# The last third of the last product of a decoder step, in seven products instead of eight

## The chip, the core and the metric

One core of a Trainium2 chip. The metric is device time in microseconds for one execution of the whole program. The engines are TensorE (PE: matmuls and transposes), VectorE (DVE), ScalarE (ACT) and GpSimd (POOL); SyncE (SP) issues every DMA of this kernel, in one queue and in order.

## The reference

One step of a one-layer hybrid decoder on 1024 prompt rows and 64 sample rows, 1024 wide. Attention and a state-space group run side by side, are normed and sent through one output projection; then:

```python
h = x + mixed
hn = rmsnorm(h, norm2_g)
y = h + (jax.nn.silu(hn @ w_gate) * (hn @ w_up)) @ w_down
...
y_prompt = rmsnorm(xp, final_norm_g)
```

w_gate and w_up are 1024 x 2816, w_down is 2816 x 1024, all float32. The change is in the product with w_down and in what feeds it and follows it.

## The kernel before

Rows are held as columns: two halves t = 0, 1 of 544 rows, each half two columns c of 272. A float32 product is three matmuls on a high and a low part of each operand (`mm3`, L68); ACT writes the high part and DVE the low part (`split`, L63).

`ffn` (L1704) computes gate and up in 11 pairs p of inner tiles. Each 2 x 2 block product there runs as seven products of sums of blocks. From the result `hid`, POOL makes the sums that the next product needs (`x`, for p < 8 only), and SP stores blocks and sums to DRAM (`dH`). Beside it `stationary` (L1666) lets POOL make sums of blocks of w_down, which SP stores to DRAM (`dS`).

`down` (L1797) computes the last product in eight pieces (t, d): d = 0 to 3 are blocks of 256 output columns. A piece is called (t,d) below. It has three thirds u of the inner dimension: rows 0 to 1023 (u = 0), 1024 to 2047 (u = 1), and 2048 to 2815 (u = 2: the last three pairs of inner tiles, p = 8, 9, 10). u = 0 and 1 are seven products each, of 4 x 3 matmuls, summed in seven PSUM banks z[0] to z[6]; u = 2 is eight plain block products of 3 x 3 matmuls in six steps (the table `PLAIN`), added into four of these banks. In all 84 + 84 + 72 = 240 matmuls for each (t,d).

After u = 1 the shared parts of the seven products leave the banks (`r`, `u2`, `u3`) and POOL adds them to the residual `o` (`base`, L1864); in u = 2 DVE adds the other banks (`last`, L1867). `o` has two buffers; its load `o<-dh` is issued at the start of u = 1. `close` (L1936) turns the finished `o` of one (t,d) by twelve PE transposes (`ptr`) while the next (t,d) computes, DVE multiplies by the norm's weight (`y`), ACT sums squares into a scratch tile (`junk`), SP stores `y` to DRAM (`dy`). `finish` (L1951) takes the first half's rows back during t = 1: six tiles of up to 104 rows by 1024 columns, each with a load `yf<-dy`, a POOL multiplication and a store `out_dram<-yf`, in one buffer. `ends` does the same work for the last (t,d) in the tail.

Weights come as `wr<-dS` or `wx<-dS` (two steps of weights each, 7 buffers in all), issued six loads ahead, and are split two or three steps ahead into `ws`. The hidden parts are `hs` (u = 0, 1) and `xp` (u = 2), loaded and split once per t. Instructions are written in program order and a scheduler merges them into each engine's stream, which the engine then runs in order.

## Time and profile before

| | us |
|---|---|
| median of 3 runs (1545.07 to 1552.62) | 1548.5 |
| the profiled execution | 1555.69 |
| its span in the profile | 1553.6 |
| PE busy | 1439.5 (93%) |
| DVE busy | 1090.4 (70%) |
| POOL busy | 729.1 (47%) |
| `ffn`, about | 850 to 1281 |
| `down` with its tail | 1281 to 1553.6 |

Times in rows are microseconds from the span's start. PE counts as busy from the first to the last cycle of overlapping matmuls, so a busy PE can still run at a lower clock; the granted clock (PEclk) is given as a share of full speed. A row's bracket tells how long the engine idled before it and what ended that.

### The profile page before, as it was taken

The numbers are of one execution on the slowest core, as the hardware profiler recorded it, in microseconds if no ns is written. First come the engines' busy times: TensorE is split into PE (matmuls) and PEld (weight loads), VectorE is DVE, ScalarE is ACT, GpSimd is POOL, SyncE is SP. The second block draws the span as 40 slices with busy tenths as digits, with TensorE's granted clock in tenths as the row PEclk, the third lists the DMA queues.
The fourth block names the chain that finished last, engine by engine and source line by source line (L and its number), as shares of the span: only waits on it lengthen the run. The fifth ranks groups of instructions, "written<-read, shape, count | busy, mean of one in ns | idle before, by whom it ended". The sixth has DMA issues, their size and how long they took to land.

```text
span 1553.6 us, 28199 instructions
## 1 busy us (share of the span) xinstructions
PE 1439.5 (93%) x10005; PEld 1344.9 (87%) x10005; DVE 1090.4 (70%) x2226; ACT 716.1 (46%) x1815; POOL 729.1 (47%) x719
## 2 busy tenths in 40 slices
PE   5988987978889999999997999999999989999996
PEld 5987977966777677789987999999999989999996
DVE  6896399958867787787989555555555577579564
ACT  6233343435467667575444333333232365466443
POOL 3058445417735454410147678788774421113331
PEclk9998988968789999889998999999999999999998
DMA  8438887799676873444342276566564368689874
GB/s 215 160 120 279 242 241 220 209 214 224 179 189 180 206 182 89 127 146 128 108 131 80 84 214 212 175 205 196 184 197 141 108 248 294 195 297 324 238 234 126
DMA packets 244187, 292.90 MB, mean 189 GB/s; under 512 B 29870, under 2 KB 185358, under 8 KB 244046
## 3 DMA queue, kind: packets, MB, share of 16 engines
q1 hardware_dynamic: 244046, 291.10, 62.7%
q8 instruction: 79, 1.29, 0.4%
q14 instruction: 62, 0.51, 0.1%
HBM read 211.69 MB, written 79.35 MB: 187 GB/s over the span
## 4 chain that ended last, share of the span: by engine, by line
PE 60%; DVE 11%; DMA 7%; issue 4%; ACT 2%; POOL 1%; SPq 1%; POOLq 0%; DVEq 0%; ACTq 0%
PE pmm L72 15%; PE pmm L70 15%; PE pmm L71 15%; PE psd L75 5%; PE pmm L75 3%; PE ptr L79 2%; PE ppo L75 2%; DVE kk L682 1%; SPq L82 1%; DMA kk<-in_cache_attn_k_dram 1%; DVE ws L65 1%; PE ptr L75 1%; DMA hs<-dH 1%; DMA kf<-in_cache_attn_k_dram 1%; DVE hn L65 1%
## 5 line engine op out<-in xcount | busy, mean ns | idle before, releaser
L70 PE MATMUL pmm<-hn,ws 128*128 128x272 f32 x1232 | 359.1, 292 | 9.1 <-DVE u L1775 4.6
L72 PE MATMUL pmm<-hn,ws 128*128 128x272 f32 x1232 | 358.2, 291 | 2.1 <-DVE ws L65 2.1
L71 PE MATMUL pmm<-hn,ws 128*128 128x272 f32 x1232 | 356.9, 290 | 0.8 <-DVE hn L65 0.8
L64 ACT ACTIVATE ws<-wr 128x512 fp32r<-128x512 f32 (+2 forms) x238 | 151.8, 645 | 207.4 <-PE pmm L72 191.0
L70 PEld LDWEIGHTS pmm<-hn,ws 128*128 128x128 f32 x1232 | 234.1, 190 | 10.5 <-DVE u L1775 4.8
L65 DVE TENSOR_TENSOR ws<-wr,ws 128x512 fp32r<-128x512 f32 (+2 forms) x238 | 202.4, 857 | 52.7 <-ACT ws L64 51.3
L72 PEld LDWEIGHTS pmm<-hn,ws 128*128 128x128 f32 x1232 | 233.6, 190 | 2.9 <-DVE ws L65 2.7
L71 PEld LDWEIGHTS pmm<-hn,ws 128*128 128x128 f32 x1232 | 234.1, 190 | 1.3 <-DVE hn L65 1.2
L70 PE MATMUL pmm<-hs,ws 128*128 128x272 f32 x448 | 131.5, 294 | 5.1 <-DVE hid L1772 5.1
L72 PE MATMUL pmm<-hs,ws 128*128 128x272 f32 x448 | 131.2, 295 | 0.5 <-DVE ws L65 0.5
L71 PE MATMUL pmm<-hs,ws 128*128 128x272 f32 x448 | 131.3, 294 | 0.0
L1779 POOL TENSOR_TENSOR hid<-hid,s 128x272 f32<-128x272 f32 x88 | 82.2, 941 | 55.9 <-DVE hid L1772 52.0
L65 DVE TENSOR_TENSOR ws<-st,ws 128x512 fp32r<-128x512 f32 x72 | 60.6, 842 | 59.0 <-ACT ws L64 58.8
L828 POOL TENSOR_TENSOR vs<-vr,vs 128x512 fp32r<-128x512 f32 x40 | 56.0, 1406 | 85.3 <-ACT vs L826 75.1
L681 POOL TENSOR_TENSOR kf<-kf,qb 128x1024 f32<-128x1024 f32 x24 | 59.1, 2471 | 73.0 <-DMA kf<-in_cache_attn_k_dram 37.3
L70 PEld LDWEIGHTS pmm<-hs,ws 128*128 128x128 f32 x448 | 86.1, 192 | 5.3 <-ACT hs L64 5.3
L72 PEld LDWEIGHTS pmm<-hs,ws 128*128 128x128 f32 x448 | 85.5, 192 | 0.9 <-DVE ws L65 0.8
L71 PEld LDWEIGHTS pmm<-hs,ws 128*128 128x128 f32 x448 | 86.0, 192 | 0.0
L64 ACT ACTIVATE ws<-st 128x512 fp32r<-128x512 f32 x72 | 45.3, 629 | 81.0 <-PE pmm L72 69.9
L1125 DVE CUSTOM_DVE_ANT_0 P<-pmm,lnc 128x256 f32<-128x256 f32 (+1 forms) x128 | 47.4, 376 | 41.9 <-PE pmm L75 33.6
L70 PE MATMUL pmm<-mT,ws 128*128 128x272 f32 x256 | 74.5, 298 | 1.4 <-ACT ws L64 1.4
L71 PE MATMUL pmm<-mT,ws 128*128 128x272 f32 x256 | 74.9, 295 | 0.0
(441 smaller groups left out, 4088.3 us busy)
## 6 DMA issues: line engine op xcount, KB each, us to landing
vr<-in_cache_attn_v_dram SPq DMA_DIRECT2D x80, 256.0 KB
wr<-dS SPq DMA_DIRECT2D x32, 512.0 KB
hs<-dH SPq DMA_DIRECT2D x28, 544.0 KB
kf<-in_cache_attn_k_dram SPq DMA_DIRECT2D x48, 256.0 KB
wr<-in_ffn_w_gate_dram SPq DMA_DIRECT2D x24, 512.0 KB
wr<-in_ffn_w_up_dram SPq DMA_DIRECT2D x24, 512.0 KB
wx<-dS SPq DMA_DIRECT2D x24, 512.0 KB
dH<-hid SPq DMA_DIRECT2D x22, 544.0 KB
```

The lines of the kernel that those rows point to most:

```text
L64: self.nc.scalar.activation(hi, src, AF.Copy)
L65: (eng or self.nc.vector).tensor_tensor(out=lo, in0=src, in1=raw(hi), op=OP.subtract)
L70: nc.tensor.matmul(out, lhsT=wh, rhs=xh, start=start, stop=False)
L71: nc.tensor.matmul(out, lhsT=wh, rhs=xl, start=False, stop=False)
L72: nc.tensor.matmul(out, lhsT=wl, rhs=xh, start=False, stop=stop)
L75: self.nc.tensor.matmul(out, lhsT=w, rhs=x, start=start, stop=stop)
L79: self.nc.tensor.transpose(out, in_, self.ident[:n, :n])
L82: return self.nc.sync.dma_start(out=out, in_=in_).ins
L681: nc.gpsimd.tensor_tensor(out=kf[i], in0=kf[i], in1=qb[b][:, 0:1].to_broadcast((128, 2, 512)), op=OP.mult)
L828: eng.tensor_tensor(out=s[:, 1], in0=vr[i], in1=raw(s[:, 0]), op=OP.subtract)
L1125: V.tensor_tensor_reduce(out=P[h, g].rearrange("p b k -> p (b k)")[:, o:o + n], in0=s[:, o:o + n], in1=lnc[:, part, 256 - n:256], scale=-1 ...
L1779: self.mark = G.tensor_tensor(out=o, in0=o, in1=sb, op=OP.mult).ins
```

## The change

u = 2 becomes seven products too, of 3 x 3 matmuls: 84 + 84 + 63 = 231 matmuls for each (t,d), in the same seven banks, which now stay open over all three thirds. For that:

- `ffn` makes the sums `x` for p = 8, 9, 10 as well: four POOL subtractions of 128 x 272 and one store `dH<-x` for each of 3 pairs and 2 halves.
- `stationary` runs the four POOL operations for u = 2 that u = 0 and 1 have, in place of one; `dS` grows from 74 to 77 blocks.
- `third(t, j)` loads and splits seven `xp` tiles for each t in place of four.
- All evacuations (`r`, `u2`, `u3`, `u4`, `base`, `last`) stand in u = 2, with j in the order 0, 1, 2, 3, 6, 4, 5; all `base` additions of the last (t,d) are on DVE, before only one of four.
- Buffers: `o` one instead of two, loaded at the start of u = 2; weights five instead of seven, issued four loads ahead instead of six; `u4` reuses `r`; `junk` is gone and the squares are written in place in PSUM.
- `finish` works on tiles of 512 columns: twelve loads, multiplications and stores in place of six.

```diff
-PLAIN = (((2, 0, 0, 0),), ((2, 0, 1, 0),), ((6, 0, 0, 0),), ((6, 0, 1, 0), (4, 1, 0, -1), (4, 1, 1, 0)), ((5, 1, 0, 0),), ((5, 1, 1, 0),))
+ORD = (0, 1, 2, 3, 6, 4, 5)
...
+XB, OB = 1, 1
...
-            dH = [[self.dram.tile([7, 128, 4, HW] if u < 2 else [4, 128, 3, HW], F32, name=f"dH{t}{u}") for u in range(3)] for t in range(2)]
+            dH = [[self.dram.tile([7, 128, 4 if u < 2 else 3, HW], F32, name=f"dH{t}{u}") for u in range(3)] for t in range(2)]
...
-            self.dS = [self.dram.tile([128, 74, 128], F32, name=f"dS{d}") for d in range(4)]
+            self.dS = [self.dram.tile([128, 77, 128], F32, name=f"dS{d}") for d in range(4)]
...
-                    if u == 2:
...
-                        G.tensor_tensor(out=S, in0=R[:, 0:3], in1=R[:, 3:6], op=OP.subtract)
...
+                    G.tensor_tensor(out=S[:, 1], in0=R[:, 0, 1], in1=R[:, 1, 1], op=OP.add)
+                    G.tensor_tensor(out=S[:, 0], in0=S[:, 1], in1=R[:, 0, 0], op=OP.subtract)
+                    G.tensor_tensor(out=S[:, 2], in0=R[:, 1, 0], in1=S[:, 0], op=OP.subtract)
+                    G.tensor_tensor(out=R[:, 0, 1], in0=R[:, 0, 0], in1=R[:, 0, 1], op=OP.subtract)
...
-                strassen = p < 8
...
-                if j == 5 and strassen:
+                if j == 5:
...
-                    if strassen:
-                        G.tensor_tensor(out=z["x"][:, 2], in0=ob[:, 2], in1=z["x"][:, 1], op=OP.subtract)
-                        self.store(d[:, 4:7], z["x"][:, 0:3])
-            yield [(0, j)] + [(1, k) for k in range(7) if j == 6] if p == P - 1 and m == "u" else ()
-
+                    G.tensor_tensor(out=z["x"][:, 2], in0=ob[:, 2], in1=z["x"][:, 1], op=OP.subtract)
+                    self.store(d[:, 4:7], z["x"][:, 0:3])
...
-                if u == 1:
-                    HO[t, d] = self.dpx[2].tile([128, 2, 2 * HW], F32, tag="o", name="o", bufs=2)
+                if u == 2:
+                    HO[t, d] = self.dpx[2].tile([128, 2, 2 * HW], F32, tag="o", name="o", bufs=OB)
...
+                R[k] = (dp.tile([128, 8, 128], F32, tag="wx", name="wx", bufs=XB) if k % (4 + XB) > 3 else
+                        wraw().rearrange("p a (b c) -> p (a b) c", b=2))[:, :b - a]
...
+                if j % 2 == 0:
+                    wload(k + 3 + XB)
...
+        def third(t, j):
+            x = HS[t, 2, j] = self.dpx[j > 3].tile([128, 2, 3, HW], F32R, name="xp", tag=f"xp{j}", bufs=1)
+            self.load(raw(x[:, 1]), dH[t][2][HN[j]])
+            self.cuts.append((self.step, x[:, 0], x[:, 1], raw(x[:, 1]), None))
...
+            if (t, d, u) == (0, 0, 0):
+                third(0, j)
...
-                (V if (t, d, u) == (1, 3, 2) else G).tensor_tensor(out=o[:, m, HW * c:HW * c + HW], in0=o[:, m, HW * c:HW * c + HW], in1=b, op=OP.add)
+                (V if (t, d) == (1, 3) else G).tensor_tensor(out=o[:, m, HW * c:HW * c + HW], in0=o[:, m, HW * c:HW * c + HW], in1=b, op=OP.add)
...
+            x = HS[t, u, j]
+            nq = 4 if u < 2 else 3
+            for q in range(nq):
+                self.mm3(z[j], W[n][:, 0, q], W[n][:, 1, q], x[:, 0, q], x[:, 1, q], u == 0 and q == 0, u == 2 and q == nq - 1)
...
-            if (u, j) == (1, 0):
-                r = dp.tile([128, HW], F32, tag="r", name="r", bufs=1)
-                nc.scalar.activation(r, z[0], AF.Copy)
-                base(0, 0, r)
-            elif (u, j) == (1, 1):
-                u2 = temp("u2", r, 1)
-            elif (u, j) == (1, 3):
-                u3 = temp("u3", u2, 3)
-                base(1, 0, u3)
-                base(1, 1, u3)
-            elif (u, j) == (2, 1):
-                last(0, 0, 2)
-            elif (u, j) == (2, 3):
-                u4 = temp("u4", u2, 4)
-                base(0, 1, u4)
-                last(1, 1, 4)
-            elif (u, j) == (2, 5):
-                last(0, 1, 5)
...
+                if j == 0:
+                    r = dp.tile([128, HW], F32, tag="r", name="r", bufs=1)
+                    nc.scalar.activation(r, z[0], AF.Copy)
+                    base(0, 0, r)
+                elif j == 1:
+                    u2 = temp("u2", r, 1)
+                elif j == 2:
+                    last(0, 0, 2)
+                elif j == 3:
+                    u3 = temp("u3", u2, 3)
+                    base(1, 0, u3)
+                    base(1, 1, u3)
+                elif j == 6:
+                    last(1, 0, 6)
+                elif j == 4:
+                    u4 = temp("r", u2, 4)
+                    base(0, 1, u4)
+                    last(1, 1, 4)
+                else:
+                    last(0, 1, 5)
...
-                elif j in (3, 5):
-                    plain(1, j == 5)
-            if t == 1 and d == 3 and u == 0 and j == 6:
+                else:
+                    third(1, j)
...
-            junk = dp.tile([128, 256], F32, tag="junk", name="junk", bufs=1)[:m]
-            nc.scalar.activation(junk, p, AF.Square, accum_out=ss[:m, i, d:d + 1])
+            nc.scalar.activation(p, p, AF.Square, accum_out=ss[:m, i, d:d + 1])
...
-            y = dp.tile([128, 1024], F32, tag="yf", name="yf", bufs=1)[:m]
-            self.load(y, dy[t0:t0 + m])
-            for _ in range(4):
-                yield
-            self.nc.gpsimd.tensor_scalar(y, y, rs, None, op0=OP.mult)
-            self.store(self.O[0][0, t0:t0 + m], y)
-            for _ in range(4):
+            for h in (slice(0, 512), slice(512, 1024)):
+                y = dp.tile([128, 512], F32, tag="yf", name="yf", bufs=1)[:m]
+                self.load(y, dy[t0:t0 + m, h])
+                for _ in range(4):
+                    yield
+                self.nc.gpsimd.tensor_scalar(y, y, rs, None, op0=OP.mult)
+                self.store(self.O[0][0, t0:t0 + m, h], y)```

SP's queue where `down` begins, before: hidden blocks of the last pairs go to `dH`, a weight load and the first `xp` loads follow. (`dH_6979` and `dH_6982` are the third u = 2 of t = 0 and 1, `dS_6985` is d = 0.)

```order
L85 DMA dH_6979<-hid 128x4x272
L82 DMA wx<-dS_6985 128x1024 x2
L85 DMA dH_6982<-hid 128x4x272
L82 DMA wx<-dS_6985 128x1024
L82 DMA gf<-in_final_norm_g_dram 128x256
L82 DMA xp_14621<-dH_6979 128x816
L82 DMA xp_14623<-dH_6979 128x816
L82 DMA wr<-dS_6985 128x768
```

The same place after:

```order
L86 DMA dH_6979<-hid 128x4x272
L83 DMA wx<-dS_6985 128x1024
L83 DMA gf<-in_final_norm_g_dram 128x256
L86 DMA dH_6979<-x 128x3x272
L86 DMA dH_6982<-hid 128x4x272
L83 DMA o<-dh_6969 128x2x544
L86 DMA dH_6982<-x 128x3x272
L83 DMA wr<-dS_6985 128x768
L83 DMA xp<-dH_6979 128x816
L83 DMA wr<-dS_6985 128x768
L83 DMA xp<-dH_6979 128x816 x2
```

The stores of POOL's sums for both halves and the load of `o` now stand ahead of the first weights and the first `xp` of the third.

SP's queue in the second half, between (1,0) and (1,2), before. (`dy_6983` holds the rows of t = 0, `dy_6984` those of t = 1; `dS_6987` is d = 2; `dh_6974` is the residual of (1,1), `dh_6975` that of (1,2).)

```order
L85 DMA out_dram<-yf 96x1024
L85 DMA dy_6984<-y 80x256
L82 DMA wr<-dS_6987 128x1024
L82 DMA yf<-dy_6983 80x1024
L85 DMA dy_6984<-y 104x256
L82 DMA wr<-dS_6987 128x1024 x2
L85 DMA dy_6984<-y 104x256
L85 DMA out_dram<-yf 80x1024
L82 DMA o<-dh_6975 128x2x544
L82 DMA yf<-dy_6983 104x1024
```

After, with the load of the seventh half tile (104x512) directly ahead of the residual of (1,1):

```order
L86 DMA out_dram<-yf 80x512
L83 DMA yf<-dy_6983 80x512
L83 DMA wr<-dS_6987 128x1024
L86 DMA dy_6984<-y 104x256
L83 DMA wr<-dS_6987 128x1024
L86 DMA out_dram<-yf 80x512
L86 DMA dy_6984<-y 104x256
L83 DMA wr<-dS_6987 128x1024
L83 DMA yf<-dy_6983 104x512
L83 DMA o<-dh_6974 128x2x544
L83 DMA wx<-dS_6987 128x1024
L83 DMA gf<-in_final_norm_g_dram 128x256
```

The half tiles stand closer together, and the residual that a (t,d) needs at its end stands behind seven of them for (1,1) and behind eleven for (1,2).

DVE at the end of the last (t,d), before (L1868 is `last`, L1865 `base`, L1972 the tail's first multiplication):

```order
L1868 TENSOR_TENSOR o<-o,pmm 128x272 x2
L1972 TENSOR_TENSOR hs<-pmm,gf 96x128 x2
L1972 TENSOR_TENSOR hs<-pmm,gf 80x128
L1874 TENSOR_TENSOR u_17899<-u_17719,pmm 128x272
L1868 TENSOR_TENSOR o<-o,pmm 128x272
L1972 TENSOR_TENSOR hs<-pmm,gf 96x128
L1865 TENSOR_TENSOR o<-o,u_17899 128x272
```

The same place after (L1858 is `last`, L1855 `base`, L1956 the tail's first multiplication):

```order
L1855 TENSOR_TENSOR o<-o,u_17929 128x272 x2
L1858 TENSOR_TENSOR o<-o,pmm 128x272
L1864 TENSOR_TENSOR r<-u_17890,pmm 128x272
L1858 TENSOR_TENSOR o<-o,pmm 128x272
L1956 TENSOR_TENSOR hs<-pmm,gf 96x128 x2
L1956 TENSOR_TENSOR hs<-pmm,gf 80x128
L1855 TENSOR_TENSOR o<-o,r 128x272
```

Three more additions to `o` are on DVE, between the last products and the tail.

## Rows read from the trace of the kernel before

**Rows 1.** The page: the chain that ended last, share of the span by engine.

```profile
PE 60%; DVE 11%; DMA 7%; issue 4%; ACT 2%; POOL 1%; SPq 1%; POOLq 0%; DVEq 0%; ACTq 0%
```

**Rows 2.** Windows: stretch, length, busy us of each engine (instructions), PEclk, DMA share, GB/s.

```profile
1000.00:1150.00 150.00, 150.00 (x1193) 150.00 (x1192) 82.15 (x148) 45.57 (x90) 116.64 (x120) 1.00 0.59 186
1200.00:1250.00 50.00, 50.00 (x400) 50.00 (x399) 27.51 (x52) 15.67 (x31) 21.04 (x19) 1.00 0.33 104
1281.00:1313.50 32.50, 32.38 (x243) 32.41 (x244) 26.59 (x38) 17.33 (x29) 6.95 (x7) 0.93 0.90 319
1313.50:1345.00 31.50, 31.50 (x255) 31.48 (x254) 18.60 (x34) 14.67 (x33) 3.37 (x4) 1.00 0.64 195
1408.00:1440.00 32.00, 31.46 (x250) 31.14 (x249) 28.75 (x51) 19.24 (x36) 13.28 (x9) 1.00 0.86 285
1440.00:1472.90 32.90, 32.36 (x259) 31.91 (x258) 18.42 (x39) 15.08 (x37) 12.87 (x10) 1.00 0.82 241
1472.90:1508.90 36.00, 33.20 (x254) 32.97 (x254) 22.41 (x38) 15.04 (x35) 11.85 (x7) 0.95 0.80 241
1508.90:1540.10 31.20, 30.91 (x248) 30.65 (x248) 17.07 (x38) 13.07 (x38) 2.59 (x3) 1.00 0.39 121
```

**Rows 3.** Timeline of PE at two places: start, us, instruction, idle before and its end.

```profile
1281.12 0.56 PE L70 MATMUL pmm<-hs,ws 128*128 128x272 f32 x1 [5.14 <-DVE hid L1772]
1479.36 0.42 PE L79 MATMUL ptr<-ident,o 128*96 128x128 f32 x2 [2.80 <-ACT junk L1946]
```

**Rows 4.** The chain, in time order, first half: start, us, what ran or was waited for.

```profile
1257.87 5.62 DMA hs<-dH
1285.31 0.23 PE pmm L72
1397.76 9.44 DMA wr<-dS
```

**Rows 5.** A window of the first half's end, columns as in group 2.

```profile
1405.00:1415.00 10.00, 10.00 (x80) 9.81 (x79) 9.33 (x15) 7.82 (x13) 3.92 (x1) 1.00 1.04 408
```

**Rows 6.** SP's timeline in the second half: stores of y, loads and stores of yf.

```profile
1428.52 0.32 SPq L85 DMA_DIRECT2D dy<-y  x1
1431.77 0.38 SPq L82 DMA_DIRECT2D yf<-dy  x1
...
1461.73 0.30 SPq L82 DMA_DIRECT2D yf<-dy  x1
...
1469.69 0.35 SPq L85 DMA_DIRECT2D out_dram<-yf  x1
...
1472.57 0.31 SPq L82 DMA_DIRECT2D yf<-dy  x1
...
1498.10 0.47 SPq L82 DMA_DIRECT2D yf<-dy  x1
```

**Rows 7.** POOL's timeline in the same stretch: the multiplication of one whole tile.

```profile
1466.82 2.85 POOL L1958 TENSOR_SCALAR yf<-yf,rs 80x1024 f32<-80x1024 f32 x1 [4.66 <-DMA yf<-dy]
```

**Rows 8.** The chain in the second half.

```profile
1426.11 0.22 PE ptr L79 x2
...
1442.02 4.35 DMA out_dram<-yf
```

**Rows 9.** Groups by line and form, POOL and DVE in `down`: busy us, mean ns.

```profile
L1865 POOL TENSOR_TENSOR o<-o,u 128x272 f32<-128x272 f32 x23 | 25.5, 1124 | 58.4 <-DVE u L1874 58.3
...
L1868 DVE TENSOR_TENSOR o<-o,pmm 128x272 f32<-128x272 f32 x32 | 13.8, 430 | 7.2 <-PE pmm L72 6.0 <-POOL o L1865 0.7
...
L65 DVE TENSOR_TENSOR xp<-xp 128x816 fp32r<-128x816 f32 x4 | 4.0, 1004 | 1.6 <-ACT xp L64 1.6
```

**Rows 10.** Groups by line and form: POOL in `ffn`, one of its sums of w_down.

```profile
L1694 POOL TENSOR_TENSOR ds<-dr,ds 128x256 f32<-128x256 f32 x16 | 15.9, 994 | 0.0
```

**Rows 11.** Groups by line and form, ACT in `down`: squares into junk, and in place in PSUM.

```profile
L1946 ACT ACTIVATE junk<-ptr 104x256 f32<-104x256 f32 x14 | 5.3, 382 | 5.7 <-DVE y L1944 5.7
...
L1973 ACT ACTIVATE pmm<-pmm 104x128 f32<-104x128 f32 x4 | 1.0, 260 | 1.1 <-DVE hs L1972 1.1
```

More of the change, by code (lines that the diff above doesn't have):

```diff
@@ new lines, in stationary @@
+                    n = 2 if u < 2 or x == 0 else 1
+                    R = dw.tile([128, 2, 2, 2, 128], F32, tag="dr", name="dr", bufs=2)[:, :, :, 0:n]
+                    S = dw.tile([128, 3, 2, 128], F32, tag="ds", name="ds", bufs=1)[:, :, 0:n]
+                    r0 = 1024 * u + 512 * x
+                    w = wd[r0:r0 + 256 * n, 256 * d:256 * d + 256].rearrange("(q h p) (w c) -> h w p q c", h=2, p=128, w=2)
+                    for h in range(2):
+                        for k in range(2):
+                            self.load(R[:, h, k], w[h, k])
@@ L1701, in stationary @@
+                    self.store(z[:, 1], S[:, 0])
+                    self.store(z[:, 5:7], S[:, 1:3])
                     yield
@@ L1799, in down @@
         V, G = nc.vector, nc.gpsimd
-        wd = I["ffn_w_down"][0]
         units = [(t, d, u) for t in range(2) for d in range(4) for u in range(3)]
-        steps = [(i, j) for i in range(len(units)) for j in range(7 if units[i][2] < 2 else 6)]
+        steps = [(i, j) for i in range(len(units)) for j in ORD]
         R, W, HO, GF = {}, {}, {}, {}
@@ L1855, in down @@
                 if u == 0:
-                    z = {k: self.bank("mm")[:, :HW] for k in (0, 1, 3, 2, 4, 6, 5)}
+                    z = {k: self.bank("mm")[:, :HW] for k in ORD}
             prep(n + LA)
+            if (t, d, u) == (0, 0, 0):
+                third(0, j)
             self.cut()
@@ L1888, in down @@
[L1888 to L1909 removed]
+                if j == 0:
[18 more added lines that the diff above has]
+                    last(0, 1, 5)
+                    if (t, d) < (1, 3):
+                        tail = itertools.chain(tail, self.close(dp, d, o, GF[t, d], SS[t], dy[t]))
+                    if (t, d) == (0, 3):
+                        fin = self.finish(dp, SS[0], dy[0])
@@ L1913, in down @@
                     self.fill(HS, dH, hnew, 1, u, j)
-                elif j in (3, 5):
-                    plain(1, j == 5)
-            if t == 1 and d == 3 and u == 0 and j == 6:
+                else:
+                    third(1, j)
+            if t == 1 and d == 3 and u == 0 and j == 5:
                 for _ in tail:
```

78 lines of the change are left out of this document (18 added, 60 removed).

## The prediction, on record before the changed kernel was run

> **What bounds the kernel now.** I read four views, in this order. The chain of waits by engine [rows 1]: 60% of it is PE, so PE's own work sets most of the time. Then the windows [rows 2]: from `ffn` to the end of `down` PE is busy 50.00 of 50.00 us, or 31.50 of 31.50 us, at full clock wherever nothing disturbs it, while POOL and DVE have room (21.04 and 27.51 of 50 us late in `ffn`, 3.37 and 18.60 of 31.50 us in `down`). 400 matmuls in 50.00 us is 0.125 us for one; I take 0.1255. So `down` is bound by PE, and a matmul that goes is worth its pitch as long as PE doesn't start to wait.
>
> The third view, PE's timeline, tells where it waits already. `down` starts with an idle of 5.14 us for DVE's `hid` [rows 3], and the granted clock is then low for a while (mean 0.93, [rows 2]): matmuls stand 0.23 us apart at 1285.31 [rows 4], that is 1.2 GHz. An undisturbed (t,d) takes 31.5 us. Of the four windows of this length class in the second half, three are longer: 32.0, 32.9 and 36.0 us, PE busy 31.46, 32.36 and 33.20 in them [rows 2]. The last holds the idle of 2.80 us for ACT's `junk` at 1479.36 [rows 3], and its mean clock is 0.95: after such an idle the clock costs as well. The later two lie where `finish` runs on POOL and SP; the first only has 0.54 us of idle, near its start, after the stretch with full DMA engines [rows 5]. The fourth view is SP's timeline there: `yf` loads follow each other 13.3 us apart on average (66.33 us from 1431.77 to 1498.10 in five steps), and a `y` store waits in the same queue behind a store that waits for POOL [rows 6, 7]. A late store holds `y`'s buffer, hence DVE, then `junk` on ACT, then PE's transposes.
>
> **The change part by part.** The sum is made against the profiled execution (1555.69 us, span 1553.6); it is 7.2 us above the median of 1548.5, and I carry the difference over to the median.
>
> *Fewer matmuls.* 9 fewer for each of eight (t,d): 72 x 0.1255 = **-9.0 us**, all on the path. An undisturbed (t,d) becomes 31.5 - 1.13 = 30.4 us.
>
> *Stalls that go.* 32.0 + 32.9 + 36.0 - 3 x 31.5 = 6.4 us. `junk` is gone, and the multiplication that a store waits for is half as long, so I let these stalls go, and the 0.5 us of the first window with them, since a wait priced below stands ahead of it: **-6.4 us**. What comes late next there is priced under the residual. Squares in place in PSUM: 0.38 us for 256 columns into `junk`, 0.26 us for 128 in place [rows 11], off PE's path either way; nothing.
>
> *Sums made earlier.* 24 more POOL subtractions in `ffn` and 8 x 3 = 24 in `stationary`, at 0.99 us or a little less each [rows 10], are 48 us over several hundred. POOL does 116.64 us in 150 at its fullest and 21.04 in 50 late in `ffn` [rows 2], with PE busy throughout: hidden, at nothing. If that cover were gone, each us would be paid. At the entry of `down` they do touch the path: DVE's last `hid` and POOL's sums run side by side there, and the stores of these sums stand in SP's queue ahead of the first weights. The bounds are 0 and 2 (two subtractions); I take **+0.7**.
>
> *The third of (0,0).* Seven `xp` tiles instead of four are loaded and split in the first (t,d). A split on DVE is 1.00 us [rows 9], and three more make 3.0; DVE has 26.59 of 32.50 us taken there [rows 2], so they nearly fit. But the first product of the third needs the last-made sums, whose store waits for POOL. Bounds 0 and 4 (the three splits and one matmul group waited for); I take **+1.3**. The weights' one more split for each (t,d) lies under PE (DVE 18.60 of 31.50 us): nothing. The weights' lead shrinks from six loads to four; a load carries two steps of 30.4/21 = 1.45 us, so some 11 us of delay in SP are still covered: nothing by itself.
>
> *The residual with one buffer.* `o<-dh` can be issued only when the last transposes of the (t,d) before have read `o`, and `base` and `last` follow. They free the bank that the next (t,d) needs with its 25th matmul. With transposes included a matmul stands for 31.5/240 = 0.131 us. At a normal border the order puts the last transposes at 183 to 195 of 231 matmuls, say 25.9 us after the (t,d)'s start. A load of this size took 5.62 us [rows 4], `base` is 1.12 and `last` 0.43 [rows 9], and 0.1 is for handing over: 33.2 us, against a due time of 30.4 + 3.3 = 33.7. It just fits: **+0.5** for (1,0) to (1,1) and +0.3 for (0,2) to (0,3), where latencies were longer. At the end of (0,3) the DMA engines are full (share 1.04, 408 GB/s [rows 5]) with the hidden blocks of the second half, and a load there took 9.44 us [rows 4]. 25.9 + 9.44 + 1.12 + 0.43 + 0.1 = 37.0 against 33.7: a wait of 0.6 (latency 6.9) to 5 us; I take **+3.3**.
>
> *The residual behind `finish`.* In the order `o<-dh` of (1,1) stands on SP right behind the load of the seventh half tile, that of (1,2) behind the eleventh. One buffer makes a chain: load, multiplication, store, next load. The second half tile can be loaded after the store of the third group of `y` in (1,0), matmul 107 there, and 2.4 us on (transposes at 1426.11, store at 1428.52 [rows 6, 8]). With a cycle c, five cycles lead from there to the seventh load, nine to the eleventh. Then come 0.4 us of issue, 5.6 for the residual, 1.1 and 0.4 for the additions and about 1 for handing over: 11 us together with the 2.4. The bank of (1,2) is due at its 25th matmul, 124 + 231 + 24 = 379 matmuls x 0.1316 = 49.9 us after matmul 107; that of (1,3) 30.4 later. So PE waits 5c - 38.9 at the first border and 9c - 69.3 in all at the second. What is c? The shortest whole cycle was 1461.73 to 1472.57, 10.84 us: 5.1 to the multiplication, 2.85 for it, 2.9 to the next load [rows 6, 7]. Half of it off the multiplication is 1.43, and 0.4 off each transfer for half the bytes: c = 8.6. From below, half of the mean cycle, 6.6; from above, the mean less the same savings, 11.0. With 8.6 the sum at the second border is 77.4 - 69.3 = **+8.1 us**, and I add **+1.0** for the clock, which fell after such waits before.
>
> A half tile's transfer need not take half the time. An output store of a whole tile took 4.35 us [rows 8]; the trace has no half one. The Trainium skill ("DMA: Bandwidth & Descriptors", section on the anatomy of one DMA on the GpSimd path) says that a DMA has a fixed part of about 2.0 us whatever its size, on another issuing path than this kernel's. By that rule, the change's six more loads and six more stores would be some 24 us of added chain, an estimate from that page, which speaks against the change; the sum with it would end with the slower rival's. Without it, a cycle that shrinks with the bytes would end with the faster one's.
>
> *The tail.* Three more `base` additions on DVE at 0.43 [rows 9] are 1.3 us between the last matmul and the transposes, and more transposes come after the last matmul. Bounds 0 and 4; I take **+2.3**.
>
> The sum: -9.0 - 6.4 + 0.7 + 1.3 + 0.3 + 3.3 + 0.5 + 8.1 + 1.0 + 2.3 = +2.1. On the median that is 1550.6, rounded to 1551 us; on the profiled execution 1557.8.
>
> **The rivals.**
>
> *Faster: the chain keeps pace.* If c is 7.7 or less, 9c - 69.3 is zero, no clock falls, and the sum is -7.0; if the border after (0,3) is hidden too, it is -10. For it: the multiplication halves for sure, and the program asks for one half tile in five steps of 30.4/21 us, 7.2 us. Against: no whole cycle was shorter than 10.84. About 1540 us.
>
> *Slower: SP's queue decides.* From c = 9.3 the chain costs over 14 us. At c = 10 (the mean cycle less the multiplication's half and most of the transfers' saving) it is 9 x 10 - 69.3 = 20.7 in place of 8.1: 1551 + 12.6 = about 1563 us. For it: loads, `y` stores and `yf` share one in-order queue, in which each one that waits holds all behind it, weights with only four loads of lead among them; the mean cycle was 2.5 above the shortest. Against: part of that mean was the program's own pace of eight steps a tile (12.6 us), not the chain.
>
> *The change does little:* stalls before stay, new ones don't come. Then -9.0 + 4.3 (entry, third, tail) is about -5, or 1544 us, inside "no difference".
>
> **How the numbers follow.** Over 0.5% (7.7 us) is what a measurement here can tell from no change. My forecast, 1551 with the small variant at 1544, has 0.44 of the chance; the faster rival 0.27, for all four new waits must stay small; the slower one 0.29. The range takes in c from about 7.5 to 10 and the bounds of the entry, the third and the tail: 1537 to 1565.
>
> **What would show it.** PE has 1848 product matmuls in `down` in place of 1920. If the steps are right, PE idles before the first matmul on a freed bank of (1,0), (1,2) and (1,3), waiting for DVE's `last`, that for POOL's `base`, and that for the load of `o`; `yf` loads stand about 8.6 us apart; and the stall on `junk` is gone. The first and the normal borders show 0 to 1 us. Wrong would be: `yf` loads at 7.2 us and PE without idle in the second half (the faster rival), or 9.5 and more with weights late too (the slower one); or a wait at every border, if a residual's load takes over 7 us everywhere.

## The result, and the profile after

The changed kernel took 1570.0 us (median of 4 runs, 1567.77 to 1575.49), the kernel before 1550.24 beside it: 1.0115 times the time, interval 1.0088 to 1.0142, some 18 us slower. The forecast was 1551 us with a range of 1537 to 1565; the result lies above it. Medians of the kernel before drift between chips and hours (1550.24 to 1555.01 in the runs below), so every run is told as a ratio to the kernel before, run beside it. (t,d), thirds and borders are named as above.

The page of after, where [rows 1] stood, and the windows of its last stage, columns as in [rows 2]:

```profile
PE 58%; DVE 11%; DMA 9%; issue 3%; POOL 2%; ACT 2%; SPq 1%; DVEq 0%; POOLq 0%; ACTq 0%
```

```profile
1274.30:1309.90 35.60, 31.41 (x211) 30.40 (x212) 29.65 (x33) 17.92 (x29) 14.70 (x12) 0.89 0.82 292
1341.30:1371.70 30.40, 30.40 (x246) 30.39 (x245) 18.20 (x35) 15.22 (x34) 5.11 (x7) 1.00 0.73 216
1401.20:1442.70 41.50, 34.53 (x252) 33.73 (x251) 34.11 (x60) 25.93 (x49) 14.28 (x11) 0.88 0.86 304
1442.70:1474.90 32.20, 30.74 (x245) 30.33 (x244) 17.80 (x37) 14.69 (x34) 10.85 (x10) 1.00 0.76 240
1474.90:1507.10 32.20, 30.77 (x245) 30.36 (x244) 18.75 (x34) 14.08 (x33) 8.86 (x8) 1.00 0.68 214
1507.10:1548.60 41.50, 32.91 (x247) 32.46 (x246) 19.22 (x38) 13.34 (x32) 6.71 (x6) 0.92 0.62 188
1548.60:1566.20 17.60, 3.20 (x12) 1.36 (x10) 7.86 (x26) 4.81 (x25) 2.17 (x2) 0.50 0.46 127
```

(0,2), the second row, is what the change was to give: 30.40 us of PE without a gap, 1.1 less than 31.50 [rows 2]. (0,0), (1,0) and (1,3) are 5 to 11 us longer than that, at a lower mean clock. PE's timeline names the waits, as in [rows 3]:

```profile
1274.29 0.56 PE L71 MATMUL pmm<-hs,ws 128*128 128x272 f32 x1 [5.36 <-DVE hid L1765]
...
1300.09 0.39 PE L71 MATMUL pmm<-xp,ws 128*128 128x272 f32 x1 [1.72 <-ACT ws L65]
...
1408.38 0.42 PE L73 MATMUL pmm<-hs,ws 128*128 128x272 f32 x1 [1.76 <-DVE ws L66]
1415.28 0.42 PE L80 MATMUL ptr<-ident,o 128*96 128x128 f32 x1 [4.44 <-DVE o L1858]
...
1479.18 0.31 PE L80 MATMUL ptr<-ident,o 128*96 128x128 f32 x1 [0.62 <-DVE o L1858]
...
1513.51 0.42 PE L80 MATMUL ptr<-ident,o 128*96 128x128 f32 x1 [5.23 <-DVE o L1858]
...
1547.34 0.53 PE L80 MATMUL pmm<-ident,o 128*96 128x128 f32 x3 [3.36 <-DVE o L1858]
```

Of the waits of 4.44, 5.23 and 3.36 us each is one for DVE's last addition to the residual. They stand before a transpose of the finished `o` (`ptr`), behind 36 and 8 matmuls of the next piece and, the last, in the tail's first transposes; not before the 25th matmul on a freed bank, as forecast. The chain of waits leads back from DVE's addition, in the first two over POOL's, to a load of `o` or to the chain of `yf`:

```profile
1394.35 9.08 DMA hs<-dH
...
1403.49 8.27 DMA o<-dh
1411.92 2.80 POOL o L1855
1414.74 0.45 DVE o L1858
...
1502.41 5.03 DMA out_dram<-yf
1507.45 2.86 DMA yf<-dy
1510.50 1.56 POOL yf L1943
1512.18 0.77 POOL o L1855
1512.96 0.45 DVE o L1858
...
1541.51 4.50 DMA o<-dh
1546.09 0.30 issue
1546.53 0.33 issue
1546.85 0.43 DVE o L1858
```

To compare kernels I cut each profiled execution's last stage at the first `hs` matmul behind the `xp` matmuls in PE's timeline (some borders of [rows 2] lie 1 to 2 us later, by counted matmuls). The stage runs from the first `hs` matmul behind the entry idle to the end of the span. The lengths in a row are of one execution, the ratio is of all runs. A piece's length repeats to 1 to 2.5 us where the code is the same (compare `moved_tiles_only` with after, and (0,0) of `no_finish` with that of after), and the stage's difference to before lies up to some 5 us from what the ratio gives: 12.6 us for `residual_one_buffer_before`, whose ratio stands for 7.6. All in us:

| kernel | (0,0) | (0,1) to (0,3) | (1,0)+(1,1) | (1,2) | (1,3) | tail | stage | ratio to before (interval) |
|---|---|---|---|---|---|---|---|---|
| before | 30.8 | 94.5 | 64.8 | 36.1 | 31.9 | 14.4 | 272.5 | 1 |
| after | 35.6 | 91.2 | 73.8 | 32.2 | 41.5 | 17.6 | 291.9 | 1.0115 (1.0088 to 1.0142) |
| moved_tiles_only | 35.1 | 92.0 | 72.2 | 31.3 | 43.2 | 16.6 | 290.4 | one run, 1570.79 us |
| two_residuals | 37.7 | 92.0 | 67.4 | 39.0 | 32.2 | 18.4 | 286.7 | 1.0107 (1.0068 to 1.0146) |
| two_residuals_adds_on_dve | 39.1 | 92.0 | 68.1 | 33.2 | 34.6 | 19.5 | 286.4 | 1.0097 (1.0065 to 1.0130) |
| both_mends | 36.3 | 92.1 | 67.7 | 32.4 | 33.9 | 21.4 | 283.7 | 1.0074 (1.0049 to 1.0099) |
| finish_on_pool_queue | 39.5 | 92.0 | 67.4 | 32.2 | 30.5 | 26.8 | 288.5 | 1.0083 (1.0046 to 1.0121) |
| pool_as_second_queue | 36.3 | 91.2 | 75.9 | 38.6 | 30.5 | 22.2 | 294.8 | 1.0110 (1.0081 to 1.0139) |
| no_finish | 37.9 | 91.2 | 72.8 | 30.4 | 31.8 | 17.8 | 282.0 | 1.0028 (0.9997 to 1.0059) |
| last_stores_from_pool | 36.3 | 92.3 | 72.1 | 35.6 | 41.3 | 16.5 | 294.2 | 1.0125 (1.0098 to 1.0152) |
| third_not_from_sums | 38.1 | 92.1 | 77.3 | 33.3 | 36.0 | 18.5 | 295.2 | 1.0147 (1.0091 to 1.0203) |
| no_sums_of_last_pairs | 29.6 | 92.0 | 73.9 | 31.6 | 37.5 | 18.1 | 282.8 | 1.0038 (1.0011 to 1.0065) |
| residual_one_buffer_before | 31.0 | 94.5 | 73.6 | 38.3 | 33.4 | 14.2 | 285.1 | 1.0049 (1.0016 to 1.0081) |
| lead_four_before | 31.1 | 94.4 | 67.8 | 36.7 | 31.9 | 13.8 | 275.7 | 1.0005 (0.9976 to 1.0034) |
| halves_before | 30.9 | 94.6 | 63.9 | 38.6 | 32.3 | 15.7 | 275.9 | 1.0011 (0.9984 to 1.0038) |
| all_cuts_before | 30.9 | 94.4 | 73.3 | 35.5 | 38.4 | 14.3 | 286.8 | 1.0074 (1.0041 to 1.0106) |
| four_y_before | 31.1 | 94.7 | 65.0 | 33.0 | 31.9 | 14.1 | 269.7 | 0.9968 (0.9941 to 0.9996) |

After against before: +4.8, -3.3, +9.0, -3.9, +9.6 and +3.2, together +19.4 us, as much as the whole loss. So it lies in this stage. (The two spans differ by 12.6 us only, 1566.2 and 1553.6: the stage began at 1274.3 in the one and 1281.1 in the other. This start lies anywhere from 1269 to 1282 in the executions of the table, with either kernel.)

### The profile page after: what moved, and what is told of

The parts are those of the page before. It is cut to its first block, busy times and chain, and to the rows that moved or that the text cites. A ratio compares the mean times of both kernels' runs of the same rounds, so it can differ in the third digit from the quotient of the medians.

```text
span 1566.2 us, 28294 instructions
## 1 busy us (share of the span) xinstructions
PE 1442.8 (92%) x9933; PEld 1342.7 (86%) x9933; DVE 1092.6 (70%) x2243; ACT 725.1 (46%) x1829; POOL 770.3 (49%) x770
## 4 chain that ended last, share of the span: by engine, by line
PE 58%; DVE 11%; DMA 9%; issue 3%; POOL 2%; ACT 2%; SPq 1%; DVEq 0%; POOLq 0%; ACTq 0%
PE pmm L73 14%; PE pmm L71 14%; PE pmm L72 14%; PE psd L76 6%; PE pmm L76 4%; PE ptr L80 2%; PE ppo L76 2%; DMA yf<-dy 2%; DMA hs<-dH 2%; DMA out_dram<-yf 1%; DVE ws L66 1%; DMA kf<-in_cache_attn_k_dram 1%; PE ptr L76 1%; POOL yf L1943 1%; DMA o<-dh 1%
## 5 line engine op out<-in xcount | busy, mean ns | idle before, releaser
L71 PE MATMUL pmm<-hn,ws 128*128 128x272 f32 x1232 | 359.4, 292 | 8.9 <-DVE u L1768 4.4
L73 PE MATMUL pmm<-hn,ws 128*128 128x272 f32 x1232 | 358.0, 291 | 2.1 <-DVE ws L66 2.1
L72 PE MATMUL pmm<-hn,ws 128*128 128x272 f32 x1232 | 357.0, 290 | 0.5 <-DVE hn L66 0.5
L65 ACT ACTIVATE ws<-wr 128x512 fp32r<-128x512 f32 (+2 forms) x279 | 175.7, 637 | 224.4 <-PE pmm L73 206.1
L66 DVE TENSOR_TENSOR ws<-wr,ws 128x512 fp32r<-128x512 f32 (+2 forms) x279 | 231.3, 834 | 64.2 <-ACT ws L65 61.7
L71 PEld LDWEIGHTS pmm<-hn,ws 128*128 128x128 f32 x1232 | 234.0, 190 | 10.7 <-DVE u L1768 4.7
L73 PEld LDWEIGHTS pmm<-hn,ws 128*128 128x128 f32 x1232 | 233.6, 190 | 2.9 <-DVE ws L66 2.7
L72 PEld LDWEIGHTS pmm<-hn,ws 128*128 128x128 f32 x1232 | 234.1, 190 | 1.0 <-DVE hn L66 0.9
L73 PE MATMUL pmm<-hs,ws 128*128 128x272 f32 x448 | 133.9, 300 | 4.1 <-DVE ws L66 4.1
L71 PE MATMUL pmm<-hs,ws 128*128 128x272 f32 x448 | 132.6, 297 | 5.4 <-DVE hid L1765 5.4
L72 PE MATMUL pmm<-hs,ws 128*128 128x272 f32 x448 | 133.2, 298 | 0.0
L1772 POOL TENSOR_TENSOR hid<-hid,s 128x272 f32<-128x272 f32 x88 | 85.1, 974 | 48.0 <-DVE hid L1765 48.0
L66 DVE TENSOR_TENSOR ws<-st,ws 128x512 fp32r<-128x512 f32 x72 | 61.7, 858 | 58.5 <-ACT ws L65 58.5
L71 PEld LDWEIGHTS pmm<-hs,ws 128*128 128x128 f32 x448 | 87.2, 195 | 5.6 <-ACT hs L65 5.5
L73 PEld LDWEIGHTS pmm<-hs,ws 128*128 128x128 f32 x448 | 87.1, 195 | 5.0 <-DVE ws L66 5.0
L72 PEld LDWEIGHTS pmm<-hs,ws 128*128 128x128 f32 x448 | 87.4, 195 | 0.0
L65 ACT ACTIVATE ws<-st 128x512 fp32r<-128x512 f32 x72 | 45.3, 629 | 80.4 <-PE pmm L73 71.8
L71 PE MATMUL pmm<-mT,ws 128*128 128x272 f32 x256 | 73.6, 294 | 1.4 <-DMA wr<-in_w_out_dram 1.4
L72 PE MATMUL pmm<-mT,ws 128*128 128x272 f32 x256 | 74.2, 293 | 0.0
```

The costliest lines, as they stand in the source:

```text
L65: self.nc.scalar.activation(hi, src, AF.Copy)
L66: (eng or self.nc.vector).tensor_tensor(out=lo, in0=src, in1=raw(hi), op=OP.subtract)
L71: nc.tensor.matmul(out, lhsT=wh, rhs=xh, start=start, stop=False)
L72: nc.tensor.matmul(out, lhsT=wh, rhs=xl, start=False, stop=False)
L73: nc.tensor.matmul(out, lhsT=wl, rhs=xh, start=False, stop=stop)
L1772: self.mark = G.tensor_tensor(out=o, in0=o, in1=sb, op=OP.mult).ins
```

## Experiments: the residual's buffer, finish and POOL's order

`two_residuals` and its control `moved_tiles_only`. Both put `yf` and `y` into idle buffers (tag `st`); the first has OB = 2 besides.

```diff
-XB, OB = 1, 1
+XB, OB = 1, 2
-            y = dp.tile([128, 256], F32, tag="y", name="y", bufs=2)[:m]
+            y = self.spare[1][:m, 256 * (i % 2):256 * (i % 2) + 256]
-                y = dp.tile([128, 512], F32, tag="yf", name="yf", bufs=1)[:m]
+                y = self.spare[0][:m]
```

> The changed kernel with two buffers for the residual o again (OB = 2). To find room, yf and the two y tiles lie in weight buffers that are idle in this stage; the work is the same. Theory A (one residual buffer, loaded behind the last transposes and behind what SP's in-order queue holds, is the main cost): the idles of 4.44, 1.45, 0.62, 5.23 and 3.36 us before DVE's additions to o go, and with them the slow clock behind three of them and part of the tail; 1570 falls by 18 to 24, to about 1548. Theory B (the chain of twelve half tiles on POOL and SP is the main cost): the last two borders keep their waits, only the one after (0,3) goes; 1570 falls by 6 to 9, to about 1562. Theory C (late weights and the crowded DMA engines around the first half's end): the idles for ws and a wait at the border after (0,3) stay; the fall is under 6.

> The changed kernel with yf and y in the idle weight buffers, still one residual buffer: the control for the first run. All theories: 1570 within 4 us, the same five waits.

The control showed the waits of after, but for a shorter one at the border after (1,0). With two buffers (1,0)+(1,1) became 6.4 us shorter and (1,3) 9.3, yet (1,2) took 6.8 more and (0,0) 2.1, and the time hardly moved. Theories A and B missed. The fall is under 6 us, as theory C had it, and a wait for `ws` of 2.43 us stayed in (1,0); but what kept the time up lies in (1,2), which C doesn't explain. The new wait, first PE, then POOL:

```profile
1482.63 0.45 PE L80 MATMUL ptr<-ident,o 128*96 128x128 f32 x1 [6.31 <-DVE o L1859]
```

```profile
1472.10 0.76 POOL L1856 TENSOR_TENSOR o<-o,r 128x272 f32<-128x272 f32 x1
1479.34 1.56 POOL L1944 TENSOR_SCALAR st<-st,rs 80x512 f32<-80x512 f32 x1 [6.48 <-DMA st<-dy]
1480.87 1.92 POOL L1856 TENSOR_TENSOR o<-o,u 128x272 f32<-128x272 f32 x2
```

POOL runs in order: the additions `o<-o,u` stand behind a multiplication that waits 6.48 us for its load. What had waited for the residual's load now waits for `yf`'s.

`no_finish` leaves finish out (the first half's rows are not written).

```diff
-                next(fin, None)
+                pass
```

> The changed kernel without the work that takes the first half's rows back (finish: loads of yf, multiplications, output stores of the first 544 rows are left out). One residual buffer as in the changed kernel. Theory A: the wait after (0,3) stays at 4 to 5 us with its slow clock and so does the one before the tail; the borders after (1,1) and (1,2) lose theirs, since the residual's load then has nothing to stand behind: about 1570 - 9 = 1561. Theory B: all waits in the second half go, and it is 1552 or less.

The border after (0,3) kept its wait (5.38 us for DVE's `o`), the last two lost theirs, as theory A said; the wait ahead of the tail shrank to 0.26, more than it said. 9.9 us of the stage hang on finish; by the two ratios the time fell by 0.87%, some 13 us, between A's 9 and B's 18.

`residual_one_buffer_before` is the kernel before with `bufs=1` for `o`.

> The kernel before with one buffer for the residual in place of two, nothing else. Its evacuations stay in two places and its eight plain products stay. Theory A says that the single buffer alone makes waits at the borders of the second half: 8 to 20 us slower than the kernel before, 1558 to 1570. Theory B and C: within 4 us of it.

0.5% slower, 12.6 us in the stage, and 8.8 of them in (1,0)+(1,1), where after lost 9.0. After has 18 matmuls less there, so it is 13.0 us over an undisturbed 60.8, this kernel 10.6 over 63.0: the single buffer is enough for most of the loss at that border, with no seven products. The waits there are ones for `ws` (0.72, 1.36 and 0.72 us) and then one of 2.88 ahead of a transpose: not the residual alone comes late. The load for (0,3) goes out at 1391.31, where the DMA engines are full, and lands 9.35 us later; in before it went out at 1364.28, ahead of the hidden blocks. The load for (1,0) has landed at 1436.33, and POOL adds it behind a multiplication of `yf` (1435.12 to 1437.97). How the waits for `ws` follow from the one buffer is not shown. (1,2) has a wait of 3.73 us for DVE's `o` besides.

`two_residuals_adds_on_dve` takes POOL's order out of it.

```diff
-                (V if (t, d) == (1, 3) else G).tensor_tensor(
+                (V if t == 1 else G).tensor_tensor(
```

> The kernel with two residual buffers, and in the second half the base additions to o on DVE in place of POOL, where they stood behind the multiplications of yf. Theory D (two causes in a row: one residual buffer, and the additions queued on POOL behind a multiplication that waits for its load): no wait over 1 us for DVE's o after (1,0); (1,1), where two_residuals took 38.1 us, falls to 30.4 to 31.5 and (1,2) to 30.4 to 31; the time is 8 to 11 us below two_residuals. Theory E (SP's in-order queue with its yf loads and stores delays the weights): the waits come back before ws, less than 4 us are gained.

Theory D held for its place: no wait for `o` after (1,0), and (1,2) fell from 39.0 to 33.2. (1,1) took 31.3 us, (1,2) stayed 2 us above its forecast. The time did not follow: 1.0097 for 1.0107. The whole stage did not gain: the next in line came up, waits for squares of `ptr` (1.84 and 1.74 us) and one of 2.51 behind a small sum on DVE, (1,3) 2.4 us longer, (0,0) and the tail too.

`finish_on_pool_queue` has finish's loads and stores issued by POOL in that kernel.

```diff
-                self.load(y, dy[t0:t0 + m, h])
+                self.nc.gpsimd.dma_start(out=y, in_=dy[t0:t0 + m, h])
-                self.store(self.O[0][0, t0:t0 + m, h], y)
+                self.nc.gpsimd.dma_start(out=self.O[0][0, t0:t0 + m, h], in_=y)
```

> The kernel with two residual buffers and the additions on DVE, and the loads and stores of finish (yf) issued by POOL, which then has nothing else to do in the second half, in place of SP. Theory E2 (y stores and weights wait in SP's in-order queue behind a yf load or an output store that itself waits): the waits for squares of ptr and for rs in the second half (2.51, 1.84 and 1.74 us there) go, (1,2) and (1,3) fall from 33.2 and 34.6 us to 30.4 to 31.5; 4 to 8 us less than two_residuals_adds_on_dve. Rival: they come from DVE and ACT being late by themselves; under 2 us.

(1,3) fell to 30.5 us, as theory E2 had it, and (1,2) to 32.2, 0.7 above its range, with one wait of 1.71 left. But nothing clear of the noise was gained in all, for finish now ends behind the last products, and POOL's sums for the tail stand behind it:

```profile
1547.71 0.52 POOL L1941 DMA_DIRECT2D st<-dy  x1 [1.98 <-DMA out_dram<-st]
1550.42 1.55 POOL L1944 TENSOR_SCALAR st<-st,rs 64x512 f32<-64x512 f32 x1 [2.19 <-DMA st<-dy]
1552.42 0.56 POOL L1945 DMA_DIRECT2D out_dram<-st  x1 [0.45 <-POOL st L1944]
1553.01 1.73 POOL L1918 TENSOR_TENSOR rs<-rs,mhalf 128x3 f32<-128x3 f32 x2
```

## Experiments: the first piece

`last_stores_from_pool` has the stores of the last pair issued by POOL; `both_mends` is that with two residual buffers and the additions on DVE.

```diff
-                    self.store(d[:, 0:4], ob)
+                    put = self.store if p < P - 1 else (lambda o, i: G.dma_start(out=o, in_=i))
+                    put(d[:, 0:4], ob)
```

> The changed kernel with the four stores of the last pair of inner tiles to dH (hid and x, both halves) issued by POOL, right behind its own sums, in place of SP. Theory F (SP's queue, held at these stores until POOL is done, makes weights and xp of (0,0) late): (0,0) falls from 36.6 us to 32.5 to 34, the waits for ws at the fifth and eighth microsecond of the stage go; 3 to 4 us less than the changed kernel. Theory G (POOL's sums themselves are late, each 1.8 us beside DVE): xp still comes late, under 1.5 us are gained.

> The first and the second kernel of this group in one. If the gains add up, D and F give 12 to 15 us below two_residuals, about the time of the kernel before or a little under it; by E and G it stays 8 us or more above the kernel before.

Theory F fell: (0,0) took 36.3 us. The two mends together show the lowest ratio of the changed kernels that do the whole work, 0.74% above before (`finish_on_pool_queue`, at 0.83%, cannot be told from it); that is about 11 us over before, not under what D and F promised but where E and G had it.

`third_not_from_sums` also reads the `xp` tiles from data that is ready long before (another third of the hidden blocks, so the sums are made and stored but not used).

```diff
-            self.load(raw(x[:, 1]), dH[t][2][HN[j]])
+            self.load(raw(x[:, 1]), dH[t][1][HN[j]][:, 0:3])
```

> The kernel with the last stores issued by POOL, and the xp tiles of both halves read from the second third of the hidden blocks, which is in DRAM long before, in place of the sums that POOL has just made. The same loads, splits and matmuls run; the third of the inner dimension is not the right one. Theory G (the sums are late on POOL, each 1.8 us, so xp comes late, and the weights' splits queued on ACT behind it): (0,0) falls from 36 to 31.5 to 33 us. Rival H (the shorter lead and the splits of seven tiles fill DVE and ACT): (0,0) stays at 35 to 37.

Still 38.1, so it looked as if theory G had fallen too. SP's timeline says otherwise: the first `xp` loads went out at 1284.44 only, the last four at 1295.44, and nothing was issued between 1272.5 and 1284.4. The data was there; the tiles' room, I take it, was not, since it is shared with the tiles that POOL was still summing and storing: the first load followed the end of POOL's last multiplication for `hid` by 0.03 us. The next run takes the sums away as well, and leaves the stores of `hid` on SP.

```profile
1272.12 0.42 SPq L83 DMA_DIRECT2D gf<-in_final_norm_g_dram  x1
1284.44 1.29 SPq L83 DMA_DIRECT2D xp<-dH  x3
...
1295.44 1.98 SPq L83 DMA_DIRECT2D xp<-dH  x4
```

`no_sums_of_last_pairs`:

```diff
-                if j == 5:
+                if j == 5 and p < 8:
...
+                    if p < 8:
```

> The changed kernel without the sums x of the last three pairs (24 POOL subtractions and 6 stores are left out) and with the xp tiles read from the second third of the hidden blocks: the loads, splits and matmuls of seven products stay, the third is not the right one. Theory G2 (the sums on POOL at the entry make xp late, by their data or by the room of their tiles, and hold SP meanwhile): (0,0) falls from 35.6 us to 31 to 33, 4 to 6 us less than the changed kernel. Theory H (shorter lead, full DMA engines, splits of seven tiles): (0,0) stays at 35 or more.

(0,0) fell to 29.6 us, and its window is full:

```profile
1273.20:1302.90 29.70, 29.68 (x221) 29.70 (x221) 27.22 (x36) 19.49 (x30) 4.71 (x6) 0.92 0.90 324
```

Seven `xp` tiles, their splits and the shorter lead fit under PE. The sums, with their stores and the late tiles, cost the 6 us. The whole kernel came down by more, 0.77% by the two ratios or some 12 us (the intervals allow 6 us either way); 4.0 of the stage's 9.1 lie in (1,3), and why is not shown. In after the sums ran like this on POOL, SP and ACT:

```profile
1279.12 1.82 POOL L1777 TENSOR_TENSOR x<-hid,x 128x272 f32<-128x272 f32 x1
1280.90 1.82 POOL L1777 TENSOR_TENSOR hid<-hid 128x272 f32<-128x272 f32 x1
...
1285.74 1.09 POOL L1781 TENSOR_TENSOR x<-hid,x 128x272 f32<-128x272 f32 x1
```

```profile
1286.86 0.84 SPq L86 DMA_DIRECT2D dH<-x  x1
1287.79 0.55 SPq L83 DMA_DIRECT2D wr<-dS  x1
1288.39 1.05 SPq L83 DMA_DIRECT2D xp<-dH  x1
```

```profile
1295.12 0.89 ACT L65 ACTIVATE xp<-xp 128x816 fp32r<-128x816 f32 x1 [3.65 <-DMA xp<-dH]
```

The sums end 12.5 us into the stage; from the stage's start SP sends one weight load (at 1279.60), and the next weights and all `xp` only after the sums' last store; and ACT, in order, has the weights' splits behind the late `xp`. Moving the wait off SP did not help, because `xp` itself was late.

## Experiments: the room, and the stalls before

`lead_four_before` is the kernel before with `wload(n // 2 + 4)` and one `wx` buffer; `halves_before` has finish's loop of the changed kernel; `all_cuts_before` has both and one buffer for `o`.

> The kernel before with weight loads issued four ahead in five buffers, as in the changed kernel, in place of six ahead in seven. Theory C (the shorter lead makes weights late where the DMA engines are full, around the end of (0,3)): 3 to 8 us slower, with waits for ws at the start of (1,0). Theory A and D: within 2 us, since 11 us of delay are still covered.

> The kernel before with finish in halves of 512 columns, twelve loads, multiplications and stores in place of six; nothing else. My forecast let the stalls of 6.4 us in the second half go with it: 3 to 6 us faster. Rival: a half tile's cycle is two thirds of a whole one, the twelve make SP's queue wait longer in all: 2 to 8 us slower, with (1,2) at 36 us or more.

> The kernel before, with its eight plain products, and the three things that were cut to make room: one residual buffer, weights four ahead in five buffers, finish in halves. If the room made for the seven products is what costs, and the costs add up (12.6, 3 and 3 us in the stage, alone), it is 13 to 20 us slower than the kernel before, (1,0) and (1,1) together 74 to 78 us in place of 64.8. If they hide each other, 8 to 12 us. If the seven products themselves cost, under 8.

The shorter lead alone cannot be told from no change in time; in the profile (1,0)+(1,1) took 3.0 us more, the low end of theory C. Halves alone did nothing for the time either, and took no stall away, against my forecast: the one in (1,2) grew to 4.91 us, on `junk` as before. All three cuts together cost 0.74% (0.41 to 1.06), 11.5 us, the second case of the expectation; in the stage of the one execution it is 14.3 us, the low end of the first. (1,0)+(1,1) shows 73.3 there, no more than one residual buffer alone: these costs hide each other; (1,3) shows 38.4, with the wait of 3.57 us before the tail that after had too.

So by the stages the room that was made costs 14.3 us, the sums at the entry 6, the tail 3, and the products give 9: +14 of the +19 measured. No run separates the other 5. Nor does one move the evacuations into u = 2, or the order of the seven products, by itself.

`pool_as_second_queue` is every mend in one: two residual buffers, all base additions on DVE, and the last stores, the second half's `xp` loads and finish issued by POOL.

> All mends in one: two residual buffers, all base additions on DVE, and POOL issues what used to hold SP's queue: the last stores to dH, the xp loads of the second half, and finish. By theories E2 and F the borders after (0,3), (1,1) and (1,2) lose their waits: 8 to 14 us less than both_mends, or 4 us below to 4 us above the kernel before. If the shorter weight lead and the full DMA engines rule there, (1,0) and (1,1) stay at 67 us together and the sum stays 5 us or more above the kernel before.

It missed: (1,0)+(1,1) at 75.9 and (1,2) at 38.6, with waits for `ws` of 3.36 and 3.42 us and for the squares of `ptr` of 4.38. There, with the DMA engines at a share of 1.03 in both kernels, four weight loads issued from 1390.11 to 1397.46 took 13.5 to 16.6 us to land; in `both_mends`, where SP issues the `xp` loads, the ones of that stretch took 6.0 to 9.1. More loads in flight where the DMA engines are full left the weights later.

`four_y_before` asks where the kernel before loses its 6.4 us.

```diff
-            y = dp.tile([128, 256], F32, tag="y", name="y", bufs=2)[:m]
+            y = self.spare[i % 4 // 2][:m, 256 * (i % 2):256 * (i % 2) + 256]
...
-            nc.scalar.activation(junk, p, AF.Square, accum_out=ss[:m, i, d:d + 1])
+            nc.scalar.activation(p, p, AF.Square, accum_out=ss[:m, i, d:d + 1])
```

> The kernel before with four y tiles in place of two, in weight buffers that are idle in this stage, and the squares in place in PSUM as in the changed kernel. If the stalls of 6.4 us in its second half come from a y store that stands in SP's queue behind an output store, with both y tiles taken: (1,1) and (1,2) fall from 32.8 and 36.1 us to 31.5 to 32.5, 3 to 6 us faster than the kernel before, faster than both. If POOL's additions or the residual's load hold PE there, within 2 us.

0.32% faster than before (0.06 to 0.59), 5 us, the fastest of all. (1,2) fell from 36.1 to 33.0 us at full clock, 0.5 above the range of the expectation; (1,1) did not fall (33.0 for 32.8). The time gained is what was expected, the stage of this execution gives 2.8 us of it:

```profile
1463.00:1496.00 33.00, 31.86 (x257) 31.64 (x255) 21.41 (x35) 14.85 (x34) 12.51 (x8) 1.00 0.80 229
```

## Why the prediction was wrong, step by step

Over undisturbed pieces (30.4 us; for (0,0) before's 30.8 less 1.1) after took 5.9 us in (0,0), 0.1 in (0,1) to (0,3), 13.0 in (1,0)+(1,1), 12.9 in (1,2)+(1,3) and 3.2 in the tail. Forecast for these were 2.0, 0.3, 3.8, 9.1 and 2.3. With 9.0 for the matmuls and 6.8 for before's own stalls taken off, that is +19.3, the measured +19.4 but for rounding, in place of +2.1. So the steps that failed are the border after (0,3), the first piece, and the residual of (1,3), which had no term.

**Matmuls, -9.0: right.** 30.37 against 31.51 us in (0,1) to (0,3)'s undisturbed pieces.

**Stalls that go, -6.4: wrong reason.** `halves_before` keeps them, and stalls on the squares of `ptr` come in kernels without `junk` too (1.84 and 1.74 us in `two_residuals_adds_on_dve`). The prediction's chain, from a late `y` store over `y`'s buffer, is not the one behind the longest stall either. The trace of before shows DVE's `y` waiting there for the norm's weight `gf`, which has one buffer:

```profile
1472.97 0.36 SPq L82 DMA_DIRECT2D gf<-in_final_norm_g_dram  x1
```

```profile
1451.01 0.42 DVE L1944 TENSOR_TENSOR y<-ptr,gf 96x256 f32<-96x256 f32 x1 [3.19 <-DMA gf<-in_final_norm_g_dram]
...
1478.32 0.42 DVE L1944 TENSOR_TENSOR y<-ptr,gf 96x256 f32<-96x256 f32 x1 [3.71 <-issue]
```

The first row stands ahead of PE's idle of 0.37 us at 1452.05, the second ahead of that of 2.80. The second names no releaser, but `gf` landed at 1478.24 and the store that held the `y` tile at 1469.79. (In `halves_before` it landed at 1479.37, and `y` began at 1479.54, ahead of the stall of 4.91.) The load of `gf` had stood in SP's queue behind the `yf` load of 1472.57, and that behind an output store. (`lead_four_before` has the forecast chain: its stall of 3.39 us ends with the landing of a `y` store.) `four_y_before` takes away most of the longest stall, but it changes the `y` tiles and `junk` together, and DVE waits 4.6 us for `gf` in it too; what a second buffer for `gf` is worth no run tests. In after the stalls don't show while PE waits for the residual, and come back when that is mended.

**Entry, +0.7: right** (5.36 us idle for 5.14 in [rows 3]). **Third of (0,0), +1.3 within 0 to 4: mis-sized,** 6.0 by `no_sums_of_last_pairs`. I priced the sums as hidden POOL work and the third as three splits. The price was a delay: most of the last pair's sums run at 1.7 to 1.8 us there in place of under 1 [rows 10], end 12.5 us into the stage, and everything in two in-order queues waits with them. "PE was busy throughout" was read from windows in the middle of `ffn`; its last pair has no cover, and that is where the sums are needed.

**Border after (0,3), +3.3 within 0.6 to 5: mis-sized,** with the next border (+0.5) 13.0 us over an undisturbed 60.8 in (1,0)+(1,1). PE's wait for the residual is 4.44 us of that, inside the bounds, though by another sum: it was due later, at the 37th matmul, and came later. The last transposes began at 1397.3, the load went out at 1403.49 and took 8.27 us, near the 9.44 I took. In between SP's queue moved only as earlier transfers landed: just ahead of this load it waited for the `hs` load of 1394.35, eight issues before, which took 9.08 us. I counted the load's latency, not its place in SP's queue. What I had at nothing is the rest: PE's waits for `ws` of 0.77 and 1.76 us, behind weight loads that took 9.83 and 9.18 us (the second landed at 1408.30, and ACT's split began at 1408.41), a clock that fell after these waits (mean 0.54 from 1408.40 to 1410.80, ahead of the long wait), and 1.45 us for the residual of (1,0) in (1,1). "11 us of delay are covered" did not hold there; `lead_four_before`, with the lead alone, shows waits for `ws` of 0.77 and 1.05 us and no change in time.

**Behind finish, +8.1 and +1.0 for the clock: right in all, not in its parts,** the one term with a derived chain. The second `yf` load went out at 1427.68, the eleventh at 1507.45: nine cycles of 8.86 us, for 8.6. PE then waited 0.80 and 0.62 us at the first of the two borders, where 5c - 38.9 had it wait 4, and 5.23 at the second, and the clock fell after that (mean 0.92). (1,2)+(1,3) took 12.9 us over undisturbed, 9.5 without the 3.36 us told under the tail. At the second border the residual landed at 1512.01 and POOL came free of `yf`'s multiplication at 1512.06, at the first at 1475.22 and 1475.69: a second way to the same wait, POOL's order, which the prediction had not seen and which held PE up in `two_residuals` once the residual was early. That the sum fits is luck in part. The shortest half transfers in the chain, of 80 rows, were 2.32 and 2.42 us (loads) and 1.97 and 2.13 (stores), from their issue to the landing; others took up to 5.53. By the Trainium skill ("DMA: Bandwidth & Descriptors", the section on one DMA's anatomy on the GpSimd path) such a half tile of 0.16 MB has an estimate of 2.0 + 0.38 = 2.38 us. The shortest of the trace, on SP's path, agree to half a microsecond, and the twelve half tiles are not cheaper than six whole ones: 12 x 8.86 = 106 us of chain against 6 x 13.3 = 80.

**Tail, +2.3: right for the tail** (17.6 for 14.4), but a term was missing: (1,3)'s own residual, issued at 1541.51 behind the last transposes and behind a load of `y` rows, which had waited for their store to land (1541.06): 3.36 us of idle just before the end. I had gone through four of the five borders.

The slower rival named the right queue with a wrong measure: it wanted c above 9.3; c was 8.86, and the time came out slower than its 1563 through the borders and the first piece.

## What to carry to other kernels

What is taken away to make room is part of the price: here a second buffer, two loads of lead and half a tile cost as much as the 72 matmuls gave, or more, and one kernel that cuts only these shows it (11.5 us by its ratio, 14.3 in its stage, for 9). A load that waits in an in-order queue, for a buffer or for the landing of earlier transfers, delays whatever stands behind it, so look for its place in the queue before its latency, at every border and at the last one too. Work counted as hidden must be checked where it is needed, not where the engine has room; and where several waits lie in a row, mending one shows the next.
